# Two-layer hybrid RWKV-7 / GLA backbone: the state sum of the first layer as an identity product in PSUM

## The chip, the cores and the metric

One core of a Trainium2 chip runs the whole program. The time is the device time of one execution in microseconds (us). The engines are PE (TensorE: matrix products), DVE (VectorE), ACT (ScalarE), POOL (GpSimd) and SP (SyncE, which issues the DMAs). Products are written to PSUM, everything else lives in SBUF.

## What is computed

The reference runs two layers over 512 latent and 256 context tokens of width 1024. In each layer a combined projection feeds an RWKV-7 branch (8 heads of 64) and a gated linear attention (GLA) branch, both scanned forwards and backwards; the branches are merged, and a squared-ReLU MLP follows. In the first layer the context tokens go through everything too; in the second they only feed the scan states. The recurrence that the change concerns is this one, per head, with a 64x64 state:

```
def step(s, inp):
    r_t, w_t, k_t, v_t, kk_t, a_t = inp
    sa = jnp.einsum("bhvk,bhk->bhv", s, kk_t)
    s = (s * w_t[:, :, None, :]
         - sa[..., None] * (kk_t * a_t)[:, :, None, :]
         + v_t[..., None] * k_t[:, :, None, :])
    return s, jnp.einsum("bhvk,bhk->bhv", s, r_t)
```

## The kernel before, in words

Everything is held feature by token, 128 features on the partitions. A wide ("dense") projection is done in float32 accuracy with three products of a high and a low part each (`sh`, `sl` by `wh`, `wl`, into tiles `d`); weights stream in from HBM and are split by ACT (`wh`) and by POOL or DVE (`wl`).

The RWKV scan is done in chunks of 64 tokens. The eight heads of a layer are four pairs (one head on partitions 0 to 63, the other on 64 to 127), and the 12 chunks are three groups of four. A pair and a group make a unit. For each unit `rw_A1` and `rw_A2` make the decays and scaled keys, `rw_B` the products inside a chunk and, in `inverse`, the inverse of a triangular matrix by five doubling levels of 64x64 products in half precision (tiles `Q`, `XY`, `i`), and `rw_C` carries the state through the four chunks of the group. It carries the forward and the backward direction at once, so a group has four steps (`st` 0 to 3), and a layer has 4 x 3 x 4 of them less the last one of each pair, whose state nobody needs: 44 steps that pass a state on.

A step takes the state from the tile `zs` (ZS), multiplies it (`c<-ZS,AR`), copies the result to `pre`, multiplies by the inverse (`c<-pre,YI`), copies the result into `za` (ZA), and then makes the next state: old state plus `za` times `tk`, all of it times the decay `E`. These last lines (1362 to 1374) depend on a switch for each layer, `ACCUM` (line 101), which is off for the first layer and on for the second:

```
pr = cps.tile([P, 2, 2, 64], F32, name="c", tag="c")
for d in range(2):
    if ACCUM[l]:
        mm(fl(pr[:, d]), ident, fl(zs[:, cc[d]]), stop=False)
    mm(fl(pr[:, d]), tk[:, cc[d]], fl(za[:, cc[d]]), start=not ACCUM[l])
for h in range(2):
    hs = HS[h]
    src = pr[hs, :, h]
    if not ACCUM[l]:
        src = G([P, 2, 64], "gs", 1)[hs]
        dve.tensor_tensor(out=src, in0=pr[hs, :, h], in1=zs[hs, sl, h, :], op=ALU.add)
    dve.tensor_tensor(out=nz[hs, ns, h, :], in0=src, in1=E[hs, sl].unsqueeze(2).to_broadcast([64, 2, 64]), op=ALU.mult)
```

The order of the instructions is not that of the code. Every engine call is recorded by the class `Order` and laid out by a list scheduler, `flush`, once for each of five parts of the program (entry, mixer and MLP of the first layer, mixer and MLP of the second). It keeps a modelled clock for each engine, takes among the calls that could start first the one with the earliest due time, and puts the dense products, which have a later due time, where PE would otherwise have nothing to do. Consecutive products of one kind (same tile size, type and output tile family, up to 16) are recorded as one piece (lines 272 to 286) and are never taken apart. The engines then run their queues strictly in that order. The mixer's dense work between two steps (gates, projections of the next pair, modulation vectors `da`) is given out by the table `CFG`.

In the profile all instructions carry line 567, the line of the scheduler that issues them, so they are told apart by their tiles. `C` is the tile of constants, which holds the identity `ident`.

Of the kernel before, what the change touches and what calls it, by code (L numbers as in the profile page):

```python
# [97 lines left out]


SB = 6  # L100
ACCUM = (False, True)

CFG = {
    "nfill": ((2, 2, 0, 2, 2, 1, 1, 2, 0, 2, 2, 0, 2, 1, 1, 0, 0, 0, 0), (2, 3, 0, 2, 2, 1, 2, 2, 0, 2, 2, 0, 1, 0, 0, 1, 0, 0, 0)),
# [470 lines left out]
def hybrid_kernel(ctx: ExitStack, tc: tile.TileContext, A: dict, out: bass.AP):  # L575
# [74 lines left out]
    def mm(o, a, b, start=True, stop=True):  # L650
        pe.matmul(o, lhsT=a, rhs=b, start=start, stop=stop)
# [277 lines left out]
    def mixer(l, acts, adas, pre, early):  # L929
# [12 lines left out]
        def G(shape, tag, bufs, dt=F32, name=None):  # L942
            return grp.tile(shape, dt, name=name or tag, tag=tag, bufs=bufs)
# [385 lines left out]
        def rw_C(X, gi):  # L1329
# [10 lines left out]
            for st in range(4):  # L1340
# [22 lines left out]
# [9 lines that stand above are left out]
# [705 lines left out]
```

## Time and profile before

| what | value |
|---|---|
| three runs | 2808.75, 2814.94, 2815.92 us (median 2814.94) |
| profiled execution | 2812.3 us, its span 2810.5 us |
| state steps of the first layer | 122 to 674 us of the span |
| state steps of the second layer | 1753 to 2205 us of the span |
| PE busy, whole span | 2662.9 us (95%) |
| DVE busy, whole span | 1624.6 us (58%) |

The first and the last product that reads a state in each layer give the two stretches; between them lie the GLA part and the output of the first mixer (674 to about 1000 us), the first MLP (to about 1650 us) and the entry of the second mixer. A time for the busy share of PE is the time in which at least one product is recorded as running; products overlap in the pipeline, so the pace of PE is read from the distance between two starts, not from the length of one. PE's granted clock is written as a share of its full rate, 1.00 being the upper of its two levels.

### The profile page before, as it was taken

How to read it: one execution, taken by the hardware profiler on the slowest of the kernel's cores; microseconds unless marked ns; L12 is line 12 of the kernel's file. 1: busy time of each engine (PE TensorE's matmuls, PEld its weight loads, DVE VectorE, ACT ScalarE, POOL GpSimd, SP SyncE). 2: the span in 40 equal slices, each digit the busy share in tenths (PEclk: the TensorE clock that was granted, in tenths of full speed). 3: DMA queues.
4: the chain of work that ended last, by engine and by line, in shares of the span. 5: the costliest groups of instructions: out<-in, count | busy, mean ns of one | idle time of the engine just before them, and what ended most of it. 6: DMA issues, size and time to landing. Idle time of an engine off the chain costs nothing.

```text
span 2810.5 us, 56340 instructions
## 1 busy us (share of the span) xinstructions
PE 2662.9 (95%) x22618; PEld 2229.4 (79%) x22618; DVE 1624.6 (58%) x2996; ACT 1282.8 (46%) x2606; POOL 1179.3 (42%) x1336
## 2 busy tenths in 40 slices
PE   7999999999989999999999899999989979899998
PEld 5788878788767878888888777777777768888887
DVE  6687787886687361122223636887878687622224
ACT  5554545545553452322134545555555564533333
POOL 3653534433321642223135546554444232733335
PEclk9999999999999989999999899999999999999999
DMA  6321323232226322222223344321311126433334
GB/s 238 117 88 56 115 93 119 82 96 67 78 90 238 101 73 63 64 64 61 64 64 103 121 157 125 95 81 57 108 39 40 42 62 221 124 109 98 94 97 132
DMA packets 148437, 276.53 MB, mean 98 GB/s; under 512 B 16496, under 2 KB 25456, under 8 KB 148176
## 3 DMA queue, kind: packets, MB, share of 16 engines
q1 hardware_dynamic: 148176, 272.93, 30.7%
q8 instruction: 178, 2.92, 0.4%
q14 instruction: 83, 0.68, 0.1%
HBM read 242.85 MB, written 30.02 MB: 97 GB/s over the span
## 4 chain that ended last, share of the span: by engine, by line
PE 76%; DVE 9%; POOL 4%; ACT 4%; DMA 4%; issue 3%; SPq 0%; POOLq 0%; ACTq 0%; DVEq 0%
PE d L567 58%; PE c L567 8%; PE m L567 5%; PE i L567 4%; PE da L567 1%; POOL wl L567 1%; DVE lw L567 1%; DVE ZA L567 1%; POOL S L567 1%; POOL x L567 1%; DMA ra<-in_ada_dram 1%; DVE ZS L567 1%; ACT f L567 1%; DMA wr<-in_win_dram 1%; DVE sc L567 1%
## 5 line engine op out<-in xcount | busy, mean ns | idle before, releaser
L567 PE MATMUL d<-sh,wh 128*128 128x512 f32 (+1 forms) x3280 | 1192.0, 363 | 28.1 <-ACT f L567 10.8
L567 PE MATMUL d<-sh,wl 128*128 128x512 f32 (+1 forms) x3280 | 1138.3, 347 | 16.0 <-POOL wl L567 13.4
L567 PE MATMUL d<-sl,wh 128*128 128x512 f32 (+1 forms) x3280 | 1138.3, 347 | 3.0 <-POOL sl L567 1.7
L567 POOL TENSOR_TENSOR wl<-wr,wh 128x512 fp32r<-128x512 f32 x356 | 479.9, 1350 | 750.7 <-ACT wh L567 734.8
L567 PEld LDWEIGHTS d<-sh,wh 128*128 128x128 f32 x3280 | 629.2, 192 | 128.3 <-issue 18.1
L567 PEld LDWEIGHTS d<-sh,wl 128*128 128x128 f32 x3280 | 628.1, 191 | 99.8 <-POOL wl L567 18.7
L567 PEld LDWEIGHTS d<-sl,wh 128*128 128x128 f32 x3280 | 629.6, 192 | 69.8 <-DVE sl L567 3.8
L567 ACT ACTIVATE wh<-wr 128x512 fp32r<-128x512 f32 x580 | 362.1, 627 | 495.8 <-PE d L567 389.9
L567 DVE TENSOR_TENSOR wl<-wr,wh 128x512 fp32r<-128x512 f32 x224 | 170.9, 767 | 180.4 <-ACT wh L567 171.7
L567 DVE TENSOR_TENSOR t<-t,d 128x512 f32<-128x512 f32 (+1 forms) x101 | 58.1, 577 | 315.5 <-ACT t L567 315.5
L567 POOL TENSOR_TENSOR sl<-t,sh 128x512 fp32r<-128x512 f32 (+2 forms) x72 | 104.8, 1458 | 207.1 <-ACT sh L567 207.1
L567 DVE TENSOR_TENSOR a<-a,d 128x512 f32<-128x512 f32 (+1 forms) x80 | 44.4, 554 | 228.8 <-PE d L567 228.7
L567 ACT ACTIVATE XY<-i 128x512 f16<-128x512 f32 x192 | 108.2, 593 | 91.0 <-PE i L567 89.1
L567 ACT ACTIVATE t<-d 128x512 f32<-128x512 f32 (+1 forms) x101 | 51.4, 510 | 167.0 <-PE d L567 166.6
L567 POOL TENSOR_TENSOR LTL<-AB,LTB 64x512 f16<-64x512 f32 x48 | 61.0, 1271 | 136.3 <-DVE LTB L567 98.4
L567 POOL TENSOR_TENSOR rn<-rn,C 128x2 f32<-128x2 f32 (+2 forms) x41 | 60.2, 1468 | 119.2 <-DVE rn L567 118.5
L567 POOL TENSOR_TENSOR S<-S,q 128x256 f32<-128x256 f32 x92 | 75.7, 832 | 56.5 <-ACT q L567 53.7
L567 PEld LDWEIGHTS <-XY 64*64 64x64 f16 x1920 | 64.3, 109 | 40.5 <-issue 27.8
L567 DVE TENSOR_TENSOR Q<-i,MK 128x512 f16<-128x512 f32 x120 | 82.7, 689 | 18.3 <-PE i L567 15.5
L567 ACT ACTIVATE f<-d 128x512 f32<-128x512 f32 (+1 forms) x85 | 54.3, 647 | 82.4 <-PE d L567 65.5
L567 PE MATMUL i<-Q,XY 64*64 64x64 f16 x1920 | 80.5, 197 | 7.9 <-DVE Q L567 5.0
L567 PEld LDWEIGHTS <-LTB 128*128 128x128 f16 x1344 | 60.3, 99 | 26.9 <-issue 21.1
(258 smaller groups left out, 4193.2 us busy)
## 6 DMA issues: line engine op xcount, KB each, us to landing
wr<-in_w_dram SPq DMA_DIRECT2D x304, 256.0 KB, 2.7
wr<-in_win_dram SPq DMA_DIRECT2D x180, 256.0 KB, 2.9
wa<-in_ada_dram SPq DMA_DIRECT2D x160, 256.0 KB, 2.9
wr<-in_wmrg_dram SPq DMA_DIRECT2D x64, 256.0 KB, 3.0
ra<-in_ada_dram SPq DMA_DIRECT2D x32, 256.0 KB, 5.4
wr<-in_wout_dram SPq DMA_DIRECT2D x32, 256.0 KB, 3.2
gdr<-fg SPq DMA_DIRECT2D x20, 384.0 KB, 3.0
gdr<-fg SPq DMA_DIRECT2D x20, 256.0 KB, 2.0
```

What stands on the lines that cost most here:

```text
L567: ins = fn(*a, **k).ins
```

## The change

The switch of the first layer is turned on:

```
 SB = 6
-ACCUM = (False, True)
+ACCUM = (True, True)
```

By the lines quoted above, in each of the 44 steps of the first layer two products of the 128x128 identity with the old state are added (one for each direction), which open the sum in PSUM that the products `c<-ZA,TK` then close, and two sums on DVE (`gs<-c,ZS`, one for each half of the partitions) go. The multiplication by the decay reads PSUM (`ZS<-c,E`) where it read the SBUF tile `gs` (`ZS<-gs,E`). Over the program PE gets 88 products more and DVE 88 instructions less; nothing else is added or removed. As the scheduler sees other calls, it lays the mixer of the first layer out anew, and from there the mixer of the second too, whose calls are the same.

Three places show it. On PE, the first state step of the first layer (ZS is the old state, C the identity, ZA and TK the update; da and d are dense fill):

```order
 L567 MATMUL m<-thw,ups 128x256 x2
 L567 MATMUL m<-adt,ups 128x256 x2
-L567 MATMUL c<-ZA,TK 128x128 x2
+L567 MATMUL c<-ZS,C 128x128
+L567 MATMUL c<-ZA,TK 128x128
+L567 MATMUL c<-ZS,C 128x128
+L567 MATMUL c<-ZA,TK 128x128
 L567 MATMUL da<-wa,SC 32x128 x8
```

Two products have become four, in one piece; the identity product of the first direction stands before the first product that needs ZA, that of the second direction behind it.

On DVE at the same step (LTB and XY belong to the inverse of the next unit, acc to the modulation vectors):

```order
 L567 COPY ZA<-c 64x2x64
 L567 TENSOR_TENSOR LTB<-AB,MK 64x8x64
-L567 TENSOR_TENSOR gs<-c,ZS 64x128
-L567 TENSOR_TENSOR ZS<-gs,E 64x2x64
+L567 TENSOR_TENSOR ZS<-c,E 64x2x64 x2
+L567 TENSOR_TENSOR acc<-acc,da 128x256
```

The two sums (one for each half) are gone, and the two multiplications stand side by side.

On PE, in the middle of the first layer's state steps, the 26th of its 60 doubling levels, in the kernel before (a level is 16 + 16 products of 64x64, the last one of a unit 16; Q and XY are its operands, i its results, pre and YI a step of the state chain):

```order
L567 LDWEIGHTS Q_1421
L567 MATMUL i_1426<-XY_1413,Q_1421 64x64
L567 MATMUL c_1412<-pre_1410,YI_767 128x64 x2
L567 LDWEIGHTS XY_1413
L567 MATMUL i_1427<-Q_1421,XY_1413 64x64
```

and the same level in the changed kernel:

```order
L567 LDWEIGHTS Q_1387
L567 MATMUL i_1392<-XY_1381,Q_1387 64x64
L567 LDWEIGHTS XY_1381
L567 MATMUL i_1393<-Q_1387,XY_1381 64x64
L567 LDWEIGHTS XY_1381
```

Before, a product of full tile size stood between the two halves of the level; now the halves follow one another. In the first layer 26 of the 60 levels were parted in this way before, and 8 are now; in the second layer it is 14 before and 16 now.

## Rows read from the trace of the kernel before

**Rows 1.** The page, part 1: busy time, share of the span and instructions of each engine.
```profile
PE 2662.9 (95%) x22618; PEld 2229.4 (79%) x22618; DVE 1624.6 (58%) x2996; ACT 1282.8 (46%) x2606; POOL 1179.3 (42%) x1336
```

**Rows 2.** Stretches: start:end, length, busy us and instructions per engine, clock, DMA share, GB/s.
```profile
core 0: us, PE busy (x) PEld busy (x) DVE busy (x) ACT busy (x) POOL busy (x), PEclk, DMA share, GB/s
122.00:674.00 552.00, 541.96 (x6656) 447.93 (x6650) 445.46 (x884) 279.45 (x630) 247.85 (x315) 1.00 0.29 91
674.00:1000.00 326.00, 300.50 (x2025) 252.33 (x2025) 210.18 (x363) 158.24 (x296) 113.74 (x135) 0.94 0.35 117
1100.00:1400.00 300.00, 300.00 (x1719) 263.56 (x1718) 58.24 (x96) 77.53 (x132) 74.80 (x52) 1.00 0.21 64
1753.00:2205.00 452.00, 425.37 (x5301) 351.19 (x5301) 356.49 (x700) 248.09 (x558) 208.97 (x270) 0.98 0.22 68
```

**Rows 3.** PE in order of time, 346 to 348 us: start, length, instruction.
```profile
346.81 0.39 PE L567 MATMUL d<-sl,wh 128*128 128x512 f32 x1
347.03 0.39 PE L567 MATMUL d<-sh,wl 128*128 128x512 f32 x1
347.35 0.22 PE L567 MATMUL i<-Q,XY 64*64 64x64 f16 x2
...
347.59 0.20 PE L567 MATMUL i<-XY,Q 64*64 64x64 f16 x2
347.72 0.71 PE L567 MATMUL c<-ZS,AR 128*128 128x128 f32 x4
```

**Rows 4.** The page, part 4: shares of the chain that ended last.
```profile
PE 76%; DVE 9%; POOL 4%; ACT 4%; DMA 4%; issue 3%; SPq 0%; POOLq 0%; ACTq 0%; DVEq 0%
```

**Rows 5.** Waits of PE, 122 to 674 us: who for whom, us in total, times, longest.
```profile
PE c L567 <- DVE pre L567: 3.2, 5, 2.0
PE c L567 <- DVE ZS L567: 1.8, 3, 1.1
PE i L567 <- DVE Q L567: 1.2, 2, 1.0
```

**Rows 6.** PE in order of time at a state step of the first layer.
```profile
304.72 0.61 PE L567 MATMUL c<-ZA,TK 128*128 128x128 f32 x4
305.16 0.61 PE L567 MATMUL c<-AR,ZS 128*128 128x128 f32 x4
```

**Rows 7.** PE in order of time at a state step of the second layer.
```profile
1882.36 0.39 PE L567 MATMUL c<-ZS,C 128*128 128x128 f32 x2
1882.58 0.39 PE L567 MATMUL c<-ZA,TK 128*128 128x128 f32 x2
...
1883.25 0.40 PE L567 MATMUL i<-XY,LTB 128*128 128x64 f16 x8
```

**Rows 8.** Groups on DVE, 122 to 674 us: names, shapes, count, busy, mean ns, idle before.
```profile
L567 DVE TENSOR_TENSOR ZS<-gs,E 64x128 f32<-64x128 f32 x88 | 43.8, 498 | 3.0
...
L567 DVE TENSOR_TENSOR gs<-c,ZS 64x128 f32<-64x128 f32 x88 | 25.3, 288 | 16.9 <-PE c L567 14.9
```

**Rows 9.** Writers of ZS: count, ns least/median/most, first and last start, forms.
```profile
L567 DVE TENSOR_TENSOR ZS<-gs,E x88: 282/290/1320, 152.9 to 674.0; 64x128 f32<-64x128 f32 x88
L567 DVE TENSOR_TENSOR ZS<-c,E x88: 254/289/296, 1754.0 to 2202.8; 64x128 f32<-64x128 f32 x88
```

**Rows 10.** DVE in order of time: two successive state steps of the first layer.
```profile
299.96 0.30 DVE L567 TENSOR_TENSOR gs<-c,ZS 64x128 f32<-64x128 f32 x1
...
305.69 0.28 DVE L567 TENSOR_TENSOR gs<-c,ZS 64x128 f32<-64x128 f32 x1
```

**Rows 11.** Waits of PE, 1753 to 2205 us.
```profile
PE c L567 <- DVE ZS L567: 6.0, 10, 2.2
```

## The prediction, made before the changed kernel ran

> **What bounds the kernel now.** I read the page's busy shares first: PE is busy for 95% of the span, DVE for 58% [rows 1]. Then the chain of waits by engine: PE holds 76% of it, DVE 9% [rows 4]. Averages hide stages, so next came the busy time of each engine in the stretch that the change touches, from the first state step of the first layer to its last. There, in 552.00 us, PE is busy for 541.96 and DVE for 445.46, 81% [rows 2]. So PE's idle time is 552.00 - 541.96 = 10.0 us, under 2%, and its granted clock is 1.00, the upper level. What can be won on PE without taking products away is those 10 us and what it loses between products.
>
> Is a busy PE at its pace? The order of time shows two dense products starting 347.03 - 346.81 = 0.22 us apart, one behind the other [rows 3]. Where a change of tile size follows, the distance is longer: 347.35 - 347.03 = 0.32, so 0.10 us more; and from the last pair of 64x64 products to a product of full size it is 347.72 - 347.59 = 0.13 us, where the 64x64 pairs of that block are 0.03 apart (eight pairs from 347.35 to 347.59), again 0.10 us more. These are the only gaps of note.
>
> What does PE wait for in the 10 us? The longest totals are the copies to pre with 3.2 us, the new state ZS with 1.8 us and Q with 1.2 us [rows 5]. The state chain is thus waited for, but little. That fits the pace of the steps: two successive steps run 305.69 - 299.96 = 5.7 us apart when they come one after the other [rows 10], while 44 steps in 552 us have 12.5 us each. The chain has slack to spare on the whole and dense products fill it.
>
> **The change part by part.**
>
> Added: 88 products of a 128x128 identity with the state. The first layer has none to measure, the second has 88. There four products, identity, update, identity, update, take 1883.25 - 1882.36 = 0.89 us, 0.22 each, and the first identity product alone 1882.58 - 1882.36 = 0.22 [rows 7]. In the first layer the two update products take 305.16 - 304.72 = 0.44, also 0.22 each [rows 6]. So the cost on PE is 88 x 0.22 = 19.4 us. It lies on the engine that ends last in this stretch; nothing hides it except PE's own idle time.
>
> Removed: 88 sums on DVE of 288 ns, 25.3 us. Also, the multiplication by the decay took 498 ns on average in the first layer [rows 8], with a median of 290 and a longest of 1320; in the second, where one operand is in PSUM, the median is 289 and the longest 296 [rows 9]. So another 88 x (498 - 289) = 18.4 us of DVE time should go, 43.7 us in all, and DVE falls from 81% to about (445.5 - 43.7) / 552 = 73% of the stretch. All of it lies beside PE's work. What it is worth is bounded by what PE waits for: at best all 10.0 us of idle time, at worst nothing. I take 4 us: the 1.8 us for ZS and most of the 3.2 us for pre (DVE makes half of pre and was late for it); Q and the rest depend on ACT and PE as much.
>
> Does the state chain get shorter? From the copy of ZA on, the old path is two update products (0.44 us), two sums and two multiplications on DVE; the new one has one or two products more (the four are one piece in the queue, so the second identity product stands behind the wait for ZA, and the first too where PE comes late), 0.22 to 0.44 us, and two sums less, 0.58 us, plus up to 2 x (498 - 289) = 0.42 us of slow multiplication. The net is 0.14 to 0.78 us per step, against 12.5 us of time that it has. Behind the waiting update product stands the dense fill of PE, as before; no wait is added, since the identity product reads a state that the product `c<-ZS,AR` of the same step has read already.
>
> Moved: the scheduler lays the first mixer out anew. The order shows one thing that PE feels: the two halves of a doubling level stand apart in 8 of 60 levels instead of 26. Each such parting costs two changes of tile size, 0.10 + 0.10 us by the distances above, so 18 x 0.20 = 3.6 us are saved. The dense products done before the last step stay the same to within one weight tile, so the GLA part behind (674 to 1000 us [rows 2]) starts with the same work left, and I cost it at nothing. The second mixer has the same calls in another order, with 16 partings for 14, 0.4 us. What its waits will be can't be read from an order. PE is idle there for 452.00 - 425.37 = 26.6 us [rows 2], 6.0 of it for the new state [rows 11]. I bound the effect by half of the idle time either way, 13 us, and take 0.
>
> DMAs, weights and their splitting are the same in number, and POOL, busy for 45% of the stretch (247.85 of 552.00 [rows 2]), gets no new work; I cost them at nothing.
>
> The sum: +19.4 - 4 - 3.6 + 0.4 = +12.2 us. The profiled execution took 2812.3 us, 1.8 more than its span, and lies 2.6 us below the median of the three runs (2814.94) and inside their range. 2812.3 + 12.2 = 2824.5; I say 2824.
>
> **A rule weighed against the rows.** The busy share of PE is the ground of all this, and in the first stretch the load row of PE reads 447.93 of 552.00 us, 81%; in the stretch from 1100 to 1400 us, where PE streams dense products and is never idle, it reads 263.56 of 300.00, 88% [rows 2]. The Trainium skill (Perfetto Trace Analysis, Identifying the Most-Contended Engine) says that the matmul busy share is no good measure of room on PE and that the share of weight loading should be read in its place. By that rule PE has 19% of 552 us free and the 19.4 us would vanish in it, and the time stay at about 2812 instead of 2824; that is the rival "hidden" below. By the rows the trace agrees only in part: a stretch with no idle time reads 88%, not 100%, so most of the 19% is not room.
>
> **The rivals.**
>
> *Hidden.* PE swallows the products in its gaps: all 10.0 us of idle time go as DVE stops being late, and the 3.6 us of tile changes, so +19.4 - 10.0 - 3.6 = +5.8, and a second mixer that comes out luckier by a few us takes the rest: 2806 to 2820, around 2814, no measurable change. For it: DVE loses a tenth of its work here, and the three longest of PE's waits are for DVE [rows 5]. Against it: the copies to pre and Q that PE waits for stay, and a new order can add waits as well as take them.
>
> *Faster: the state chain decides.* If the steps of the chain set the end of the stretch, and the fill only lies between, the new products cost nothing and each step is shorter by up to 0.78 us: 44 x 0.78 = 34 us, with the 0.14 us end 6 us. In the middle that is 20 us, 2792. The point from which it decides is a step that waits in earnest: PE would show ZS waits in most steps, not 3 of 44 with 1.8 us in all [rows 5]. The Trainium skill (SBUF — State Buffer, "SBUF: two separate sides") says that a DVE instruction with two SBUF inputs and a GpSimd instruction exclude each other; the 1320 ns beside 296 agree, and they are what would make the gain large here.
>
> *Slower by more: the second mixer falls badly.* It has the same calls in a new order, less fill, and waits for the state in 10 places already [rows 11]. If its idle time grows by half, 13 us come on top: 2812.3 + 12.2 + 13 = 2838.
>
> That the change doesn't do what it says is excluded by the order: 88 products more, 88 sums less, and the multiplication reads PSUM.
>
> **How the numbers follow.** The forecast, 2819 to 2831, has a chance of 0.50; hidden 0.26; faster 0.11; the bad second mixer 0.13. No change from 2812.3 that can be told from noise means within 0.3%, 8.4 us, so up to 2820.7: of the forecast's 0.50 I put 0.07 below that edge. Slower is then 0.43 + 0.13 = 0.56; of hidden, 0.24 stay within and 0.02 fall beyond it on the fast side: within 0.31, faster 0.13. The range for 8 in 10 reaches from the middle of hidden to the end of the bad case, 2809 to 2838; it leaves out the faster rival.
>
> **What would show it.** In the changed profile 176 rows of `c<-ZS,C` (two for each product) appear in the first layer, 0.22 us apart from what follows; the stretch of the state steps grows from 552 us to about 564; PE's idle time in it is 5 to 8 us; the multiplication by the decay has a mean near 289 ns; DVE falls to about 73%; the second stretch keeps 452 us to within 13. I am wrong if the first stretch is no longer than before (then PE had room, or the chain decided), or if the time moved by more outside it than inside.

## The result, and the profile after

The changed kernel takes 2854.95 us (2846.70 to 2860.08, four runs), the kernel before 2811.85 (2807.54 to 2815.92, four runs): the ratio is 1.0147, with a 95% interval of 1.0120 to 1.0174, or about 41 us more (43 by the medians). The profiled execution took 2851.11 us with a span of 2849.3. The direction is the one forecast, the size is more than three times the +12 us, and the time lies outside the range.

The page after, part 1, in the columns of [rows 1]:

```profile
PE 2688.0 (94%) x22794; PEld 2255.7 (79%) x22794; DVE 1584.0 (56%) x2908; ACT 1280.0 (45%) x2606; POOL 1178.2 (41%) x1336
```

PE is busy for 2688.0 - 2662.9 = 25.1 us more, DVE for 1624.6 - 1584.0 = 40.6 us less. The swap of work took place about as it was worked out (19.4 us on PE, 43.7 on DVE).

By stretches, in the columns of [rows 2]: the state steps of the first layer, what follows them in the first mixer, and the state steps of the second layer:

```profile
124.00:682.00 558.00, 550.76 (x6806) 463.19 (x6805) 403.02 (x795) 276.19 (x627) 249.87 (x314) 1.00 0.28 89
682.00:1000.00 318.00, 291.35 (x2011) 244.44 (x2009) 199.62 (x343) 151.27 (x281) 109.23 (x132) 0.96 0.35 118
1763.00:2233.00 470.00, 439.91 (x5310) 359.08 (x5311) 362.86 (x703) 247.33 (x559) 209.69 (x270) 0.96 0.21 66
```

In the first layer the stretch is 558 us for 552, with 558.00 - 550.76 = 7.2 us idle for 10.0, and DVE is at 403.02 of 558.00, 72%. In the second layer, where no call has changed, it is 470 us for 452, and PE's granted clock is 0.96 for 0.98.

The writers of ZS (count, ns least, median, most; first and last start) give the two stretches to a tenth of a us. The first layer, against 152.9 to 674.0 in [rows 9]:

```profile
L567 DVE TENSOR_TENSOR ZS<-c,E x88: 255/289/296, 153.7 to 680.9; 64x128 f32<-64x128 f32 x88
```

The second layer, against 1754.0 to 2202.8:

```profile
L567 DVE TENSOR_TENSOR ZS<-c,E x88: 255/290/296, 1766.4 to 2232.6; 64x128 f32<-64x128 f32 x88
```

From the first to the last of these writes it is 680.9 - 153.7 = 527.2 us for 674.0 - 152.9 = 521.1 in the first layer, +6.1, and 2232.6 - 1766.4 = 466.2 for 448.8 in the second, +17.4. The start of the second layer's stretch has moved by 1766.4 - 1754.0 = 12.4 us, its end by 29.8 and the span by 38.8. Two thirds of the loss thus come behind the start of the second layer's steps, where the two programs have the same calls. That the other third, 12.4 us, is close to the +12 of the forecast says little: it holds the first MLP too, whose calls are the same as well, and in the profile of e1 below, where the MLP keeps its old order, 1760.2 - 1754.0 = 6.2 us of it are left.

The four products of one step in the first layer, PE in order of time (start, length, instruction):

```profile
245.66 0.38 PE L567 MATMUL c<-ZS,C 128*128 128x128 f32 x2
245.88 0.39 PE L567 MATMUL c<-ZA,TK 128*128 128x128 f32 x2
246.11 0.39 PE L567 MATMUL c<-ZS,C 128*128 128x128 f32 x2
246.33 0.39 PE L567 MATMUL c<-ZA,TK 128*128 128x128 f32 x2
```

They start 0.22 us apart, as in the second layer [rows 7]. PE's waits in the first layer's stretch, in the columns of [rows 5]:

```profile
PE i L567 <- DVE Q L567: 2.0, 4, 1.0
PE da L567 <- DMA wa<-in_ada_dram: 0.9, 2, 0.5
PE m L567 <- ACT ta L567: 0.8, 1, 0.8
PE i L567 <- ACT Q L567: 0.8, 2, 0.4
PE c L567 <- DVE pre L567: 0.5, 2, 0.4
```

The waits for ZS (1.8 us before) are gone from the list, and of the 3.2 us for pre 0.5 is left. In the second layer's stretch the longest are now

```profile
PE d L567 <- ACT f L567: 4.8, 6, 1.8
PE i L567 <- DVE Q L567: 3.2, 5, 1.0
PE c L567 <- DVE pre L567: 3.1, 6, 0.9
```

where the 6.0 us for ZS led before [rows 11].

### The profile page after: what moved, and what is told of

It is laid out like the page before. It is cut to its first block, busy times and chain, and to the rows that moved or that the text cites. A ratio compares the mean times of both kernels' runs of the same rounds, so it can differ in the third digit from the quotient of the medians.

```text
span 2849.3 us, 56617 instructions
## 1 busy us (share of the span) xinstructions
PE 2688.0 (94%) x22794; PEld 2255.7 (79%) x22794; DVE 1584.0 (56%) x2908; ACT 1280.0 (45%) x2606; POOL 1178.2 (41%) x1336
```

## The experiments

Three parts of the program after the first mixer (its MLP, the second mixer, the last MLP) have the same calls in both kernels, and only their order differs. So the order of a part can be exchanged without touching its work: the scheduler is given, for a part, the recorded order of one kernel or of the other, and places the calls engine by engine as that says. Below, `old` and `new` are the five recorded orders of the kernel before and of the changed kernel; None lets the scheduler choose, which for the entry gives the same in both. Ratios are to the kernel before, run on the same chip between them; 0.1% is 2.8 us.

**The first mixer's change alone (e1), the rest alone (e2), the second mixer alone (e3).**

```
 e1:  ACCUM = (True, True);  FORCE = [None, new[1], old[2], old[3], old[4]]
 e2:  ACCUM = (False, True); FORCE = [None, old[1], new[2], new[3], new[4]]
 e3:  ACCUM = (False, True); FORCE = [None, old[1], old[2], new[3], old[4]]
```

> Identity products on, the first mixer as in the changed kernel; the MLP of the first layer, the second mixer and the last MLP get, instruction for instruction, the order of the kernel before. Theory (the excess over the forecast is the new order of the second mixer, whose calls are the same): the time is about 12 us over the kernel before, as the change's stage and what follows up to the second mixer were at +12.6 us in the changed kernel's trace; 8 to 16. Rival (the second layer is slower for a reason that the first layer's products cause, clock or buffers, whatever its order): about +40 us, like the changed kernel.

> Identity products off and the first mixer in the order of the kernel before; everything from the first MLP on in the order of the changed kernel. Theory: +22 to +32 us over the kernel before, without any identity product in the first layer. Rival: within 5 us of the kernel before.

> The kernel before with one part alone, the second mixer, in the order of the changed kernel. Theory: it holds nearly all of the excess, +20 to +28 us, and PE shows more time at the lower clock level between 1725 and 2370 us than before (31 us there before, 65 in the changed kernel). Rival: the loss is spread over the three parts, and this one gives under +12.

Measured: e1 1.0050 (1.0032 to 1.0069), +14 us. e2 1.0098 (1.0082 to 1.0115), +28 us, without one identity product in the first layer. e3 1.0068 (1.0053 to 1.0083), +19 us. The first two add up to 1.0148, the changed kernel's 1.0147. So the swap costs 14 us, and 28 us are the price of laying out the rest anew. The theory's numbers hold; that the loss needs the products of the first layer is excluded by e2. e3 just misses its window (20 to 28).

The second layer's ZS writes of e1, in the old order,

```profile
L567 DVE TENSOR_TENSOR ZS<-c,E x88: 255/290/296, 1760.2 to 2213.7; 64x128 f32<-64x128 f32 x88
```

and of e3, in the new order:

```profile
L567 DVE TENSOR_TENSOR ZS<-c,E x88: 253/289/296, 1750.0 to 2217.0; 64x128 f32<-64x128 f32 x88
```

That is 2213.7 - 1760.2 = 453.5 us and 2217.0 - 1750.0 = 467.0. In ten profiles with the old order of the second mixer this stretch took 448.8 to 457.6 us, and in the three with the new order (the changed kernel, e2 and e3) 466.2 to 467.3: the two don't overlap. The kernel before, at 448.8, is the shortest of its ten, so some 5 of the 17.4 us above are that one execution's luck.

Is it the clock? The second stretch of e1 (old order), by the view of [rows 2],

```profile
1757.00:2214.00 457.00, 431.49 (x5304) 357.04 (x5305) 357.74 (x703) 247.83 (x558) 208.72 (x270) 0.96 0.22 68
```

and of e3 (new order):

```profile
1747.00:2217.00 470.00, 439.92 (x5309) 359.48 (x5310) 361.30 (x702) 247.58 (x558) 209.97 (x270) 0.96 0.21 66
```

Both have a granted clock of 0.96, and the new order still takes 470 us for 457. Over the wider stretch that the expectation for e3 names, the clock is lower in e3 than in the kernel before, as expected. The kernel before, then e3:

```profile
1725.00:2370.00 645.00, 593.58 (x6729) 482.68 (x6725) 516.01 (x980) 348.35 (x748) 267.74 (x348) 0.97 0.26 81
1725.00:2370.00 645.00, 587.58 (x6590) 474.26 (x6589) 499.41 (x949) 336.70 (x723) 262.49 (x343) 0.95 0.22 70
```

But in e1, with the old order, it is as low:

```profile
1725.00:2370.00 645.00, 594.29 (x6723) 483.56 (x6720) 501.10 (x960) 345.08 (x744) 270.10 (x353) 0.95 0.23 73
```

So the clock of these stretches doesn't tell the two orders apart. It has a small part in their difference: the traces of e5 and e10 (old order) and of e3 and the changed kernel (new) each show 41.0 us of the stretch between the ZS writes at the lower of PE's two levels, and the stretch takes 454.7 and 457.6 us against 467.0 and 466.2, so some 10 of the 13 us remain at equal clock.

PE's idle time is 457.00 - 431.49 = 25.5 us in e1 and 30.1 in e3, 4.6 more. The other 8.4 us are time in which some product is recorded as running, though the number of products is the same. An estimate from the starts says where they lie. Against the usual distance between two products of the same shapes at the same clock, the starts that come over 60 ns late add up to 94 to 95 us in the three profiles with the new order and to 86 to 88 in six with the old one (the kernel before, e1, e4, e5, e9, e15). That is some 8 us more, of which only about 4 show as idle time: a product that waits starts late while the one ahead is still recorded as running. What the late ones wait for is spread over many tiles.

**The products in the old order (e4), and the DVE half alone (e5).**

```
 e4:  ACCUM = (True, True); FORCE = [None, old[1] without the sums, old[2], old[3], old[4]]
 e5:  the kernel before in its order, and in the first layer
-                    if not ACCUM[l]:
+                    if False:
                         src = G([P, 2, 64], "gs", 1)[hs]
```

> Identity products on and the DVE sums gone in the first layer, but every engine keeps the order of the kernel before, in all parts. Theory (PE pays for the products, little comes back): +12 to +20 us, 19.4 us of products less some of PE's waits. Rival (PE hides them in its idle time): 0 to +6. Against the first run of this group the difference is what the new order of the first mixer gave: I expect it 3 to 6 us better than the old order.

> The kernel before in its own order, but in the first layer the DVE sums are left out and no identity product takes their place: the old state is dropped from the next one (so the values are not the reference's), and the multiplication by the decay reads PSUM. It prices the DVE half of the change alone. Theory (DVE has little that PE waits for): 2 to 8 us under the kernel before. Rival (the state chain decides): 15 us or more under it. With the products in the old order at +11.5 us, the products alone then cost 13 to 20 us.

Measured: e4 1.0041 (1.0026 to 1.0055), +11.5 us; e5 0.9989 (0.9977 to 1.0001), -3 us, with no change just inside its interval. Their stretches in the first layer, e4

```profile
L567 DVE TENSOR_TENSOR ZS<-c,E x88: 273/289/297, 152.9 to 684.9; 64x128 f32<-64x128 f32 x88
```

and e5:

```profile
L567 DVE TENSOR_TENSOR ZS<-c,E x88: 256/289/298, 153.1 to 666.2; 64x128 f32<-64x128 f32 x88
```

are 684.9 - 152.9 = 532.0 and 666.2 - 153.1 = 513.1 us. They differ only in the 88 identity products: 18.9 us, 0.215 each, against the 19.4 of the forecast. Against the 521.1 us before, dropping the sums gives back 8.0 us in the stretch, of which 3 reach the end of the program; the mean granted clock of e5's executions is 0.9747, that of the kernel before beside them 0.9768. e4 lies just under its window (12 to 20), e5 in its own. "Hidden" fell: in this stretch PE pays for the products in full, and over the program e4 and e5 are 14.5 us apart. That the chain decides fell too, with -3 us where -15 or more was its claim. On e1 against e4, the new order of the first mixer is not better over the whole: 1.0050 against 1.0041, intervals overlapping. The 3 to 6 us that were expected of it are there in the stretch, 532.0 - 525.8 = 6.2 us, but it gives them back before the second layer: from the last ZS write of the first layer to the first of the second it is 1760.2 - 678.9 = 1081.3 us in e1 and 1075.2 in e4. The writes of e1 in the first layer, for the 525.8:

```profile
L567 DVE TENSOR_TENSOR ZS<-c,E x88: 255/289/296, 153.1 to 678.9; 64x128 f32<-64x128 f32 x88
```

**The sums in the order made for the products (e6).**

```
 ACCUM = (False, True); FORCE = [None, new[1] with each sum ahead of its multiplication, old[2], old[3], old[4]]
```

> The DVE sums as before and no identity products in the first layer, but the first mixer in the order that the changed kernel has; each sum stands right ahead of its multiplication; all later parts in the old order. Theory (swap and order add up): the products in the old order cost 11 us, products and new order 14, so the new order alone is 0 to +6 us over the kernel before. Rival (the new order is good for one of them only): above +10, as DVE gets 44 us of work back that this order did not reckon with.

Measured: 1.0099 (1.0081 to 1.0116), +28 us, so the rival holds. PE's waits in the stretch begin with

```profile
PE c L567 <- DVE ZS L567: 20.5, 23, 2.0
PE i L567 <- DVE Q L567: 1.6, 3, 1.0
```

so 23 of the 44 steps wait for ZS, 20.5 us in all, against 3 with 1.8 us [rows 5]. All 23 are for the product `c<-ZS,AR`, the first of the next step. An order made for four products and two multiplications puts it too early for four DVE instructions. The state chain has slack only because the order gives it some.

**The second layer without identity products (e7 in the order made for them, e16 in a layout of its own).**

```
-ACCUM = (False, True)
+ACCUM = (False, False)
 e7:  FORCE = [None, old[1], old[2], old[3] with each sum ahead of its multiplication, old[4]]
 e16: FORCE = [None, old[1], old[2], None, old[4]]
```

> The reverse in the second layer: its identity products off, sums on DVE as in the first, every engine in the order of the kernel before. Theory (an identity product costs PE its time wherever PE is the bound): 3 to 12 us under the kernel before. Rival (in the second layer PE waits for DVE, so the products earn their time): 3 to 15 us over it.

> DVE sums in the second layer too, its mixer laid out by the scheduler for these calls, all other parts in the old order. With the sums in a layout made for products it was +43 us. Theory (in the second layer the products are worth their time at equal quality of layout): +25 to +45 us over the kernel before, above the +19 to +24 of the layouts with products. Rival (what +43 showed was only a layout made for other work): +5 to +24 us.

Measured: e7 1.0149 (1.0129 to 1.0170), +42 us, against the theory's sign: removing 88 products from PE made the program slower. e16 1.0187 (1.0163 to 1.0211), +53 us, more than either expectation. PE's waits in the second stretch of e7,

```profile
PE c L567 <- DVE ZS L567: 34.4, 29, 3.6
PE i L567 <- ACT XY L567: 4.3, 7, 1.7
```

and of e16:

```profile
PE i L567 <- DVE Q L567: 12.2, 13, 2.7
PE c L567 <- DVE ZS L567: 9.1, 10, 2.0
PE c L567 <- DVE pre L567: 6.7, 7, 2.8
```

In e7 29 of the 44 steps wait for the state, 34.4 us. In e16 the waits are spread over ZS, Q and more; the six longest are all for DVE. The stretch is 2254.2 - 1749.3 = 504.9 us there:

```profile
L567 DVE TENSOR_TENSOR ZS<-gs,E x88: 282/290/1355, 1749.3 to 2254.2; 64x128 f32<-64x128 f32 x88
```

Even against the slowest layout with products that was measured (e13 below, +36) the sums cost some 17 us more. So in the second layer the identity product earns its time, as far as one borrowed order and one layout of its own can show it, and in the first it doesn't. With sums in both layers, PE is idle for 10.0 of 552 us in the first [rows 2] and, in e7, for 488.00 - 430.55 = 57.5 us in the second, at a granted clock of 0.93:

```profile
1748.00:2236.00 488.00, 430.55 (x5100) 347.29 (x5101) 385.48 (x785) 246.03 (x554) 204.12 (x270) 0.93 0.20 62
```

That this idle time is the reason for the opposite outcome is argued from these rows; no run changes it alone.

**Other layouts of the second mixer (e8, e13, e14).** The scheduler models windows of the clock, counted from the zero of its own time. Moving that origin gives another layout of the same calls. In e8 the origin was moved while the MLP ahead was modelled, which handed the second mixer another start; in e13 and e14 it was moved in the mixer itself.

```
-        k = int(s // WIN)
+        k = int((s + PHASE) // WIN)     # e13: 1000, e14: 2000 ns in the second mixer
 FORCE = [None, old[1], old[2], None, old[4]]
```

> The kernel before with one part alone laid out anew: the second mixer by the same scheduler from the same calls, but with the origin of its modelled clock windows moved by 1000 ns. No instruction is added or removed. Theory (any other layout of that part is worse than the one that the kernel before has, by chance of the draw): +8 to +25 us, like the second mixer of the changed kernel (+19). Rival (the changed kernel's layout is a bad one, the usual one is as good as that of before): within 6 us.

> The kernel before with its second mixer alone laid out anew, the origin of the modelled clock windows moved by 1000 ns in that part. If the old layout is a good draw: +10 to +28 us, like the two layouts measured so far (+19 and +24). If those two were bad draws: within 8 us.

> The same with 2000 ns. Good draw before: +10 to +28 us. Bad draws so far: within 8 us.

Measured: e8 1.0084 (1.0067 to 1.0100), +24 us; e13 1.0128 (1.0098 to 1.0158), +36; e14 1.0052 (1.0030 to 1.0075), +15. With the changed kernel's own (e3, +19) that is four further layouts of the same calls by the same rules, all slower than the old one. e8 and e14 came in at what was expected of a good draw, e13 above it. The ZS writes of e13, the slowest,

```profile
L567 DVE TENSOR_TENSOR ZS<-c,E x88: 256/290/296, 1750.9 to 2237.2; 64x128 f32<-64x128 f32 x88
```

and of e14:

```profile
L567 DVE TENSOR_TENSOR ZS<-c,E x88: 255/289/297, 1749.8 to 2215.6; 64x128 f32<-64x128 f32 x88
```

take 486.3 and 465.8 us for the 449 to 458 of the old order. The old layout of the second mixer is a good draw, and the changed kernel drew an ordinary one. Why it is the best of five is not shown. The scheduler has settings of its own for each part (the table `SEG`); if they were chosen by the time of this layout, any other one would be worse on average, and no run here tries other settings.

**Other layouts of the first mixer, with sums (e9, e11) and with products (e10, e12).**

```
 FORCE = [None, None, old[2], old[3], old[4]]     # PHASE in the first mixer: 1000 (e9, e10), 2000 ns (e11, e12)
 e9, e11: ACCUM = (False, True);  e10, e12: ACCUM = (True, True)
```

> The kernel before (DVE sums in the first layer); its first mixer alone laid out anew by the same scheduler with the origin of the modelled clock windows moved by 1000 ns, all other parts in the old order. It shows what a new layout of the first mixer costs without the change. If the layout of the kernel before is a good draw, as e8 showed for the second mixer: +8 to +25 us. If it is a usual one: within 6 us.

> The first run of all (identity products in the first layer, later parts in the old order, +14 us), its first mixer laid out anew with the same move of 1000 ns. Theory (a product costs PE its time, whatever the layout): 8 to 15 us over the run with sums at the same move. Rival (against another layout than the lucky one the products cost nothing or gain): within 6 us of the run with sums at the same move, or under it.

> As the run with sums at 1000 ns, the origin moved by 2000 ns: +8 to +25 us over the kernel before if that has a good draw, within 6 us if it has a usual one.

> As the run with products at 1000 ns, the origin moved by 2000 ns. Theory: 8 to 15 us over the run with sums at the same move. Rival: within 6 us of it, or under it.

Measured, with sums: 1.0001 (0.9986 to 1.0016) and 0.9994 (0.9980 to 1.0007). With products: 1.0061 (1.0038 to 1.0083) and 1.0045 (1.0030 to 1.0061). The stretches by the writes of ZS, e9 (519.9 us):

```profile
L567 DVE TENSOR_TENSOR ZS<-gs,E x88: 275/290/1734, 152.7 to 672.6; 64x128 f32<-64x128 f32 x88
```

e11 (516.3 us):

```profile
L567 DVE TENSOR_TENSOR ZS<-gs,E x88: 282/290/1412, 156.0 to 672.3; 64x128 f32<-64x128 f32 x88
```

e10 (535.0 us):

```profile
L567 DVE TENSOR_TENSOR ZS<-c,E x88: 255/289/297, 153.0 to 688.0; 64x128 f32<-64x128 f32 x88
```

e12 (528.9 us):

```profile
L567 DVE TENSOR_TENSOR ZS<-c,E x88: 257/290/296, 156.3 to 685.2; 64x128 f32<-64x128 f32 x88
```

Unlike the second mixer, the first is hardly touched by the two new draws: with sums it stays within 0.1% of the old one. The products cost 0.60% at one move and 0.51% at the other, 17 us (a little over the window of 8 to 15) and 14, like the 14 of e1; in the stretch they cost 535.0 - 519.9 = 15.1 and 528.9 - 516.3 = 12.6 us. So the price of the swap isn't an accident of one layout.

**The first MLP alone in the new order (e15).**

```
 ACCUM = (False, True); FORCE = [None, old[1], new[2], old[3], old[4]]
```

> The kernel before with the MLP part of the first layer alone in the order of the changed kernel. All later parts in the new order cost +28 us and the second mixer of them +19, so the two MLP parts should hold 8 to 9; in the traces the stretch from the last GLA state to the second layer's first state is 6 to 8 us longer where this part has the new order. Expected: +4 to +10 us. Rival (the parts do not add up, the mixer's loss depends on how it is entered): within 3 us.

Measured: 1.0070 (1.0049 to 1.0090), +20 us, more than expected, and with e3's +19 more than the +28 of e2, which holds both. The excess, 11 us, is not far beyond the error of the three together, about 8. The ZS writes of e15 in the two layers show where its time lies:

```profile
L567 DVE TENSOR_TENSOR ZS<-gs,E x88: 282/290/1317, 153.6 to 676.0; 64x128 f32<-64x128 f32 x88
L567 DVE TENSOR_TENSOR ZS<-c,E x88: 255/290/297, 1761.9 to 2218.0; 64x128 f32<-64x128 f32 x88
```

From the last write of the first layer to the first of the second, where this MLP lies, it is 1761.9 - 676.0 = 1085.9 us. In the nine profiles with the old order of both the first mixer and the MLP it is 1072.6 to 1080.0, 1075.2 on average, and in e2, which has the new MLP too, 1085.6. The second layer's stretch of e15, 456.1 us, lies in the range of the old order. So the profiles put 6 to 13 us on the MLP and 13 (466.8 against 453.7, the averages) on the state steps of the second mixer, together near the 28 us of e2. They don't show that a part costs more beside one that was laid out for another neighbour, and they have no place for the rest of e15's 20 us, of which the lower clock, below, may be a part.

## Why the prediction was wrong

The first half of it, the price of the swap, held in its main term. PE bounds the first layer's stretch, and the products cost 18.9 us there (19.4 forecast). DVE fell to 72% (73% forecast) and the multiplication by the decay to a mean of 288 ns, as this group after the change shows (columns as in [rows 8]):

```profile
L567 DVE TENSOR_TENSOR ZS<-c,E 64x128 f32<-64x128 f32 x88 | 25.3, 288 | 26.4 <-PE c L567 25.5
```

The smaller terms were off. The relief of DVE was put at 4 us and is 8.0 in the stretch and 3 over the whole program: it was read from the waits that show as PE's idle time, and by the estimate from the starts the late ones fall by about 6 us from the kernel before to e5, of which only about 4 show as idle time. The new order, put at 3.6 us for fewer changes of tile size, gives 6.2 in the stretch, with the waits. And the part behind the stretch was costed at nothing, where e1 is 1081.3 - 1075.2 = 6.1 us longer than e4. So the stretch grew by 4.7 us in e1 and by 6.1 in the changed kernel (558 us by the windows, where about 564 was forecast). The sum of this half, +12.2 us, stands near the 14 (9 to 19) of e1 in part by luck, as these misses cancel; the 14 and 17 of the two other layouts, with 12.6 and 15.1 in the stretch, bear it out better.

One row was misread. The 5.7 us between two successive steps run from the second sum of one step to the first sum of the next. The first sum of the earlier step is this one,

```profile
298.13 0.28 DVE L567 TENSOR_TENSOR gs<-c,ZS 64x128 f32<-64x128 f32 x1 [0.55 <-PE c L567]
```

so a step takes 305.69 - 298.13 = 7.6 us. Against the 12.5 us that it has, the argument stands.

The rival "hidden" took the share of weight loading as the measure of room, after the Trainium skill (Perfetto Trace Analysis, Identifying the Most-Contended Engine). Read so, it fails here: the share rose only from 81% to 463.19 / 558.00 = 83%, and the 18.9 us were paid in full. The section names the arithmetic done against the peak beside that share, and this was not worked out.

The step that failed is the one on what is laid out anew: "What its waits will be can't be read from an order ... I bound the effect by half of the idle time either way, 13 us, and take 0." Two things were wrong in it. The middle of the draw isn't 0: five layouts of the second mixer were measured, and the one that the kernel had is the fastest of them; the other four cost 15 to 36 us, above the bound (for the smallest, e14, the interval reaches down to 8). And only the two mixers were spoken of, here and in the section on the change, while the order of both MLPs changes too; the first MLP was not priced at all, and alone in its new order it costs 20 us, of which its trace shows 6 to 13 in that part. Together all parts behind the first mixer cost 28 us (23 to 32) with no change in their calls. The bound from PE's idle time was also the wrong kind of bound: in e3 two thirds of the loss in the second stretch lie where PE is recorded as busy. The prediction's own sign of being wrong came: of the 38.8 us by which the span grew, 6.1 lie inside the first stretch and 32.7 outside it.

Of the rivals, "hidden" and "faster" fell to e4 and e5. "The second mixer falls badly" is what happened, at a chance of 0.13 and a price of 2838 us that was too low, for it counted one part and half its idle time. What makes one layout of the same calls faster than another was not settled. It is no single wait, and the clock is a part of it at most. Among the executions of one kernel, 0.001 less of the mean granted clock goes with about 1.5 us more, taken over all runs. The executions of e3 average 0.9740 against 0.9766 for the kernel before beside them, those of e13 and e15 0.9708 and 0.9720 against 0.9775. By an estimate from these numbers the clock holds about 4 of the 19, 10 of the 36 and 8 of the 20 us; whether the layout lowers it was not tested.

## What to carry to other kernels

A sum moved from VectorE into a PSUM accumulation cost the full issue time of its products in the layer where TensorE hardly waits, and won in the layer where TensorE would wait for that sum: read the idle time of TensorE in the stretch, and how many steps wait for the state, before copying an edit from one layer to another. Idle time alone undercounts: a product that starts late behind one still recorded as running doesn't show in it (in the second mixer's new order some 4 of 8 us did). Where a scheduler orders the program by modelled time, an edit can lay out everything behind it anew; price that as a term of its own (here nothing for two new draws of the first mixer, 15 to 36 us for four of the second), and measure the edit with the order of the rest held fixed.

## What the runs showed of the hardware

Work taken off TensorE can lower its clock, where the engine then waits. In the second layer's stretch PE is idle for 25.5 of 457 us at a granted clock of 0.96 with the products (e1), for 57.5 of 488 at 0.93 without them (e7), and in e16, by the view of [rows 2],

```profile
1746.00:2254.00 508.00, 442.97 (x5144) 358.73 (x5145) 392.00 (x790) 248.15 (x560) 208.27 (x270) 0.90 0.19 61
```

for 508.00 - 442.97 = 65.0 us at 0.90. Between profiles of one order the clock of this stretch differs by about 0.02 (0.98 in the kernel before, 0.96 in e1), so the 0.93 and 0.90 stand apart from that. The waits for DVE thus come with a second price, products run at the lower of the two levels.

The identity product of 128x128 with 128 columns in float32 costs PE 0.215 us (e4 against e5).
